# Awaiting the last five stores behind the end of the context, on semaphores of their own

## The chip, the cores and the metric

One core of a Trainium2 chip. The metric is the device time of one execution in microseconds, as a median of several executions. "Span" is the time from the first to the last instruction of the kernel in a trace; the device time is 1.3 to 1.8 us longer.

## The reference, cut to what matters

```python
W_adapted    = W + scale * (lora_A @ lora_B)              # 256 x 256
W_final      = W_adapted / sqrt(sum(W_adapted**2, 0) + 1e-8) * m
y            = x.reshape(-1, 256) @ W_final               # 32768 x 256, fp32 in and out
```

x and y have 33.55 MB each, so 67.1 MB must move between HBM and the core.

## The kernel before

The work is cut into 8 blocks of 4 MB. SyncE issues the loads and the stores; five buffers are shared by loads and stores (the result of a block overwrites its x). GpSimd rounds x to bf16, TensorE transposes it and multiplies, VectorE and ScalarE copy results. Everything stands in one critical section of the tile framework, and the engines keep in step by semaphores, counters that one engine or a transfer raises and another waits for. A transfer of x or y raises its semaphore 16 times; it has "landed" when the sixteenth increment is there. A barrier is a meeting point: no engine passes it before all have come. SyncE's stream, cut to the loads and stores of x:

```python
    ctx.enter_context(tc.tile_critical())          # line 54; closed when the function returns
    ...
    for b in range(XBUFS):                         # XBUFS = 5
        load_x(b)

    for b in range(NBLK):                          # NBLK = 8
        nc.sync.wait_ge(sem("done"), b + 1)        # ScalarE has written block b
        nc.sync.dma_start(out=rows(out_flat, b), in_=x_bufs[b % XBUFS][:]).then_inc(
            sem(f"store{b}"), 16)
        if b >= 1 and b - 1 + XBUFS < NBLK:
            nc.sync.wait_ge(sem(f"store{b - 1}"), 16)
            load_x(b - 1 + XBUFS)
    for b in range(NBLK - XBUFS, NBLK):            # the last five stores
        nc.sync.wait_ge(sem(f"store{b}"), 16)      # line 130
    ...
    with _tile.TileContext(nc) as tc:              # line 303; its exit adds the closing barriers
        tile_dora_forward_kernel(tc, *args)
```

So all stores have landed before the section is closed; then its barrier runs, then the context's: two barriers over all engines with a clear of the used semaphores between them.

Of the kernel before, what the change touches and what calls it, by code (L numbers as in the profile page):

```python
# [11 lines left out]
def kernel(  # L12
# [10 lines left out]
    nc = tc.nc  # L23
# [15 lines left out]
    NBLK = N // BLK  # L39
# [3 lines left out]
    XBUFS = 5  # L43
# [7 lines left out]



    ctx.enter_context(tc.tile_critical())

    def sb(name, shape, dtype):
        return ctx.enter_context(nc.sbuf_tensor(name, shape, dtype))
# [31 lines left out]
    n2_ps = y_ps[1][:, 0, :]  # L89
    mb_ps = y_ps[1][:, 2, :]  # L90

    sems = {}

    def sem(name):
        if name not in sems:
            sems[name] = tc.alloc_semaphore(name)
        return sems[name]
# [5 lines left out]
    def load_x(b):  # L103
        nc.sync.dma_start(out=x_bufs[b % XBUFS][:], in_=rows(x_flat, b)).then_inc(
            sem(f"load{b}"), 16
        )
# [14 lines left out]
    for b in range(NBLK):  # L121
# [4 lines left out]
        if b >= 1 and b - 1 + XBUFS < NBLK:  # L126
            nc.sync.wait_ge(sem(f"store{b - 1}"), 16)
            load_x(b - 1 + XBUFS)
    for b in range(NBLK - XBUFS, NBLK):
        nc.sync.wait_ge(sem(f"store{b}"), 16)  # L130


    nc.gpsimd.memset(zeros[:], 0.0).then_inc(sem("pool"), 1)
# [10 lines left out]
    for g in range(NCH):  # L144
        b, c = divmod(g, CH)
# [51 lines left out]
    for g in range(NCH):  # L197
        b, c = divmod(g, CH)
# [73 lines left out]
            product(c)  # L272


# [1 line left out]
_INS = ['x', 'W', 'lora_A', 'lora_B', 'm', 'scale']  # L276
_OUTS = [((16, 2048, 256), 'float32')]
# [30 lines left out]
```

## Time and profile before

| | before |
|---|---|
| device time, median | 166.26 us (166.16 to 166.46) |
| span of the profiled run | 164.3 us |
| traffic | 33.85 MB read, 33.55 MB written, 410 GB/s |
| last work of a compute engine | 139.6 us |
| last landing of a store | 162.80 us |

The page of the kernel before: the span, busy tenths of ScalarE and of the DMA engines in 40 slices, and the chain of work that ended last.

```profile
span 164.3 us, 2075 instructions
...
ACT  3010077577578577576000675027800377000000
...
DMA  5998999989999999999999999999999999999960
...
## 4 chain that ended last, share of the span: by engine, by line
PE 1%; ACT 1%; issue 0%
```

The DMA engines are busy from the second slice on, to the last but one; the compute engines have nothing left in the last six slices. The chain of this page stops at ScalarE's last copy, because it follows work of engines and not stores. The same in three stretches of the tail (the columns are named in the second line):

```profile
core 0 of [0], span 164.3 us
core 0: us, PE busy (x) PEld busy (x) DVE busy (x) ACT busy (x) POOL busy (x), PEclk, DMA share, GB/s
139.00:150.00 11.00, 0.00 (x0) 0.00 (x0) 0.00 (x0) 0.60 (x1) 0.00 (x0) 0.69 1.01 438
150.00:160.00 10.00, 0.00 (x0) 0.00 (x0) 0.00 (x0) 0.00 (x0) 0.00 (x0) 0.50 0.90 387
160.00:164.30 4.30, 0.00 (x0) 0.00 (x0) 0.00 (x0) 0.00 (x0) 0.00 (x0) 0.50 0.05 23
```

Up to 160 us the store stream is the whole matter, and after it come 4.3 us in which almost nothing moves. The waits of SyncE's queue in two windows (who waited for whom; us in total, how often, the longest; SPq and PEq are the instruction queues of SyncE and TensorE). From 139 to 150 us:

```profile
SPq L123 <- ACTq L205: 19.8, 1, 19.8
```

And from 150 us on:

```profile
SPq L130 <- DMA out_dram<-x_sb: 22.8, 2, 13.1
SPq L303 <- PEq L303: 0.8, 2, 0.6
```

Line 130 is the wait for the stores; line 303, the closing barriers, comes after it. What lies behind the last landing is too short for the page, so here is an extract of the trace's own records (start and end in us, engine, instruction, line; many left out):

```
162.799           last of the 16 increments of the last store
162.816 162.844   SyncE   semaphore wait (two of the stores)             130
162.889 162.921   SyncE   branch, with the wait for another store        109
163.044 163.061   SyncE   semaphore: the section's barrier begins         54
163.335 163.348   SyncE   the section's barrier ends                      54
163.610 163.661   TensorE semaphore: first barrier of the context ends   303
163.771 164.014   GpSimd  range clear of the semaphores                  303
164.258 164.309   TensorE semaphore: second barrier of the context ends  303
164.544 .. 165.069  nine updates of semaphore 2 (the runtime)
164.968 .. 165.633  resets of all semaphores (the runtime)
165.857 .. 166.215  nine updates of semaphore 2 (the runtime)
```

That the updates of semaphore 2 are the runtime's is from the Trainium skill, "Runtime: NRT & Kernel Launch", section "Semaphores 0–2 are reserved", which calls number 2 the sync barrier. The trace agrees so far as it goes: the kernel uses no such semaphore, and the updates come before its first instruction (the last of them within 0.001 us of it) and after its last.

Two of the 16 increments of the last store come late: fourteen are there by 160.31, the last two at 162.55 and 162.80.

### The profile page before, as it was taken

Reading aid. Unit: us, or ns where it says so; the run is one execution under the profiler, and the core shown is the slowest. Engines: PE = TensorE matmul, PEld = TensorE weight load, DVE = VectorE, ACT = ScalarE, POOL = GpSimd, SP = SyncE. Lnnn points to the kernel's source line nnn. Section 1 sums busy time; section 2 is a strip of 40 time slices with the busy share of each in tenths; the row PEclk is TensorE's granted clock in tenths of the full one; section 3 lists DMA queues with packets and bytes.
Section 4 is the critical chain, followed back from the end, with each engine's and each line's share of the span. In section 5 each row is a group of like instructions: output and inputs, shape, how many; then the busy total and the mean of one; then the engine's idle time right before and its main releaser. Section 6 shows DMA issues by size and latency. Waiting matters only on the chain. (4 is left out here: it accounts for less than half of the span.)

```text
span 164.3 us, 2075 instructions
## 1 busy us (share of the span) xinstructions
PE 99.7 (61%) x778; PEld 83.9 (51%) x778; DVE 51.2 (31%) x76; ACT 66.8 (41%) x67; POOL 66.2 (40%) x70
## 2 busy tenths in 40 slices
PE   1260899899899898994009993399704996000000
PEld 0120698798798796992007891279603895000000
DVE  0439355354453554451003450045301352000000
ACT  3010077577578577576000675027800377000000
POOL 1006859587785885800039600693007920000000
PEclk9999999999999999999555799579995799955555
DMA  5998999989999999999999999999999999999960
GB/s 199 415 479 383 499 391 415 479 383 495 399 399 359 399 479 401 439 439 399 479 407 439 447 399 457 433 423 455 407 431 439 423 463 399 439 447 407 471 295 16
DMA packets 2630, 67.45 MB, mean 410 GB/s; under 512 B 433, under 2 KB 450, under 8 KB 578
## 3 DMA queue, kind: packets, MB, share of 16 engines
q1 hardware_dynamic: 2448, 67.37, 95.9%
q10 hardware_dynamic: 178, 0.03, 0.1%
q8 instruction: 1, 0.02, 0.0%
q14 instruction: 3, 0.02, 0.0%
HBM read 33.85 MB, written 33.55 MB: 410 GB/s over the span
## 5 line engine op out<-in xcount | busy, mean ns | idle before, releaser
L150 POOL CAST xb<-x_sb 128x1024 bf16<-128x1024 f32 x64 | 65.5, 1049 | 65.2 <-DMA x_sb<-in_x_dram 50.6
L201 ACT COPY x_sb<-y_ps 128x1024 f32<-128x1024 f32 x64 | 64.8, 1013 | 64.5 <-PE y_ps L258 64.5
L258 PE MATMUL y_ps<-w_final,xt 128*128 128x256 bf16 x512 | 69.9, 282 | 3.9 <-PEq L235 3.6
L184 DVE COPY xt<-xt_ps 128x512 f32<-128x512 f32 x64 | 43.9, 691 | 77.1 <-PE xt_ps L246 77.1
L246 PE MATMUL xt_ps<-identity,xb 128*128 128x128 f32 x256 | 41.8, 295 | 28.4 <-PEq L235 28.4
L258 PEld LDWEIGHTS y_ps<-w_final,xt 128*128 128x128 bf16 x512 | 50.7, 101 | 14.7 <-issue 8.3
L246 PEld LDWEIGHTS xt_ps<-identity,xb 128*128 128x128 f32 x256 | 32.7, 153 | 31.4 <-issue 30.7
L223 PE MATMUL y_ps<-sq,ones 128*128 128x256 f32 x4 | 2.1, 674 | 1.6 <-DVE sq L169 1.6
L194 ACT ACTIVATE norm<-y_ps,eps_col 128x256 f32<-128x256 f32 x1 | 0.5, 474 | 5.9 <-PE y_ps L223 5.9
L212 PE MATMUL y_ps<-identity,a_nat 128*16 128x128 f32 x2 | 0.6, 396 | 3.6 <-DMA a_nat<-in_lora_A_dram 3.6
L180 DVE TENSOR_TENSOR w_final<-wam,rnorm 128x256 bf16<-128x256 f32 x2 | 2.3, 1200 | 0.0
L223 PEld LDWEIGHTS y_ps<-sq,ones 128*128 128x128 f32 x4 | 1.2, 323 | 2.3 <-DVE sq L169 2.1
L192 ACT ACT_TABLE_LOAD x1 | 1.3, 1283 | 2.4 <-issue 2.4
L212 PEld LDWEIGHTS y_ps<-identity,a_nat 128*16 128x16 f32 x2 | 0.1, 88 | 3.6 <-issue 3.6
L177 DVE RECIPROCAL rnorm<-norm 128x256 f32<-128x256 f32 x1 | 1.7, 1745 | 0.0
L171 DVE COPY m_all<-y_ps 128x256 f32<-128x256 f32 x1 | 0.4, 425 | 3.3 <-PE y_ps L228 3.3
L160 DVE CAST b_bf<-b_nat 16x256 bf16<-16x256 f32 x1 | 0.3, 281 | 3.6 <-DMA b_nat<-in_lora_B_dram 3.6
L216 PE MATMUL y_ps<-b_bf,aT 16*128 16x256 bf16 x2 | 0.6, 402 | 1.3 <-DVE aT L162 1.3
L228 PE MATMUL y_ps<-m_row,ones 1*128 1x256 f32 x2 | 1.2, 710 | 0.0
L216 PEld LDWEIGHTS y_ps<-b_bf,aT 16*128 16x128 bf16 x2 | 0.1, 104 | 1.8 <-DVE aT L162 1.8
L165 DVE SCALAR_TENSOR_TENSOR wa<-y_ps,w_nat 128x512 f32<-128x512 f32 x1 | 0.7, 692 | 0.8 <-PE y_ps L216 0.8
L228 PEld LDWEIGHTS y_ps<-m_row,ones 1*128 1x128 f32 x2 | 0.5, 308 | 0.7 <-issue 0.7
(12 smaller groups left out, 3.2 us busy)
## 6 DMA issues: line engine op xcount, KB each, us to landing
x_sb<-in_x_dram SPq DMA_DIRECT2D x8, 4096.0 KB, 29.3
out_dram<-x_sb SPq DMA_DIRECT2D x8, 4096.0 KB, 34.1
w_nat<-in_W_dram SPq DMA_DIRECT2D x1, 256.0 KB, 2.9
a_nat<-in_lora_A_dram ACTq DMA_DIRECT2D x1, 16.0 KB, 2.6
b_nat<-in_lora_B_dram ACTq DMA_DIRECT2D x1, 16.0 KB, 3.5
m_row<-in_m_dram ACTq DMA_DIRECT2D x1, 1.0 KB
```

The costliest lines, as they stand in the source:

```text
L150: nc.gpsimd.tensor_copy(out=xb_bufs[g % NXB][:], in_=x_bufs[b % XBUFS][:, c * J : (c + 1) * J, :],).then_inc(sem("rounded"), 1)
L165: nc.vector.scalar_tensor_tensor(out=wa[:], in0=ab_ps, scalar=float(scale), in1=w_nat[:], op0=ALU.mult, op1=ALU.add).then_inc(dv, 1)
L177: nc.vector.reciprocal(out=rnorm[:], in_=norm[:]).then_inc(dv, 1)
L180: i = nc.vector.tensor_mul(out=w_final[:, t], in0=wam[:, t], in1=rnorm[:])
L184: nc.vector.tensor_copy(out=xt_bufs[g % NXT][:].rearrange("p r t -> p (r t)").bitcast(FP32), in_=xt_ps[g % 4][:],).then_inc(sem("copied"), 1)
L192: nc.scalar.activation(out=warm[:], in_=eps_col[:], func=AF.Sqrt)
L201: nc.scalar.copy(out=x_bufs[b % XBUFS][:, c * J : (c + 1) * J, :], in_=y_ps[g % 2][:]).then_inc(sem("room"), 1)
L212: i = nc.tensor.transpose(aT_ps[:, t * P : (t + 1) * P], a_nat[:, t, :], identity[:])
L223: i = nc.tensor.matmul(n2_ps, ones[:], sq[:, t, :], start=(t == 0), stop=(t == KC - 1))
L228: nc.tensor.matmul(mb_ps, ones[0:1, :], m_row[:], start=True, stop=True).then_inc(pe, 1)
L246: i = nc.tensor.transpose(xt_ps[c % 4][:, j * P : (j + 1) * P], xb_bufs[c % NXB][:, j, :].bitcast(FP32), identity[:],)
L258: i = nc.tensor.matmul(y_ps[c % 2][:, j, :], xt_bufs[c % NXT][:, j * P : (j + 1) * P, t], w_final[:, t, :], start=(t == 0 and (j % (J // 2 ...
```

## The change

The intent: let the closing barriers run while the last stores travel, and have SyncE alone wait for the stores, behind all barriers. The context would clear and free semaphores of its own when it closes, so these five come from outside it and SyncE clears them.

```diff
-    ctx.enter_context(tc.tile_critical())
+    critical = ExitStack()
+    critical.enter_context(tc.tile_critical())
 ...
-    sems = {}
+    late = [nc.alloc_semaphore(f"store{b}") for b in range(NBLK - XBUFS, NBLK)]
+    sems = {f"store{b}": late[b - NBLK + XBUFS] for b in range(NBLK - XBUFS, NBLK)}
 ...
-    for b in range(NBLK - XBUFS, NBLK):
-        nc.sync.wait_ge(sem(f"store{b}"), 16)
 ...
+    critical.close()
+    tc.close()
+    tc.compile()
+    for s in late:
+        nc.sync.wait_ge(s, 16)
+        nc.sync.sem_clear(s)
```

## The prediction

> **What bounds the kernel now.** The DMA engines. The slices of the page show a DMA share of 0.9 to 1.0 from 5 us to 160 us; the stages view gives 1.01 and 438 GB/s in 139 to 150 us, with nothing left to compute. The traffic is 33.85 MB in and 33.55 MB out. The chain of waits on the page ends at 139.6 us, at the last ScalarE copy, because it does not follow stores; what really ends last is the store stream behind it. The DMA landings in the trace: the last store is issued at 139.66 and its sixteen increments arrive at 159.39 to 162.80 us (fourteen by 160.31, two stragglers 2.2 us later).
>
> **The tail, from the raw instruction and semaphore records.** Landing 162.80; SyncE's wait ends 162.84, its branch 162.92; the critical section's barrier (line 54) 163.04 to 163.35; first all-engine barrier (line 303) to 163.66; GpSimd clears the semaphore range 163.77 to 164.01; second barrier to 164.309, the end of the span. So 1.51 us lie between the last landing and the last instruction, all serial, all on the critical path. The Trainium skill, "Runtime: NRT & Kernel Launch", section "Semaphores 0-2 are reserved", says that semaphore 2 is the runtime's sync barrier; the trace has its updates at 164.54 to 165.07, then resets of all semaphores from 164.97 to 165.63, then again at 165.86 to 166.22. That part is behind the kernel and stays.
>
> **What the change removes, adds, moves.** No byte, no compute. SyncE leaves its stream right after issuing the last store (139.99), so the 1.4 us of closing barriers run at about 140.1 to 141.6 us, under the stores. What is left behind the last landing is one wait and one clear on SyncE. The wait took 0.044 us from landing to end of instruction; single semaphore instructions of SyncE take 17 to 32 ns and follow at about 60 ns. Estimate from these: last instruction at 162.80 + 0.04 + 0.08 = 162.92 us. The first four waits and clears are over long before (store 14 lands at 153.14). Saving in the span: 1.39 us.
>
> There should be a little more outside the span. In the old tail semaphore 2 waits about 0.17 us on its third hop (0.205 us against 0.034 to 0.044 elsewhere): a late engine. From the order of the resets (the group 207 to 255 first, at 164.97) I infer that SyncE is the turning point of this barrier. With the four others already there, only SyncE's own arrival counts. Estimate: SyncE's update about 0.25 us after its last instruction (Tensor's first took 0.235), where it was 0.59 us before: another 0.2 to 0.35 us. Total about 1.65 us.
>
> **Predicted:** 166.26 - 1.65 = 164.6 us, range 164.2 to 165.2; within 2% almost certainly (0.98), faster by over 2% 0.01, slower by over 2% 0.01. In the ratio: about 1% faster.
>
> **What would show each step right.** Span 162.8 to 163.1. The DMA queue's own waits: no wait for PEq late in the trace, the wait for the last store still at 162.8 and now the end. The records: line 54's and the closing line's barriers at 140 to 142 us. Landings of the last five stores unchanged within 0.3 us; DMA slices unchanged. Semaphore 2: hops without the 0.2 us gap.
>
> **What would make it wrong.** If SyncE's drain in the barriers waits for its outstanding DMAs, the barriers stay behind the landing and nothing is gained (166.2). No record here shows a drain with DMAs of its own queue in flight. If the clear on SyncE is as long as GpSimd's range clear (0.24 us), each costs and I lose 0.2 us. If SyncE's exit after its last instruction is slow, the extra outside the span is absent: 164.9.

## The result, and the profile after

The changed kernel takes 164.46 us (median, 164.38 to 164.72), the kernel before in the same rounds 166.35 us. The ratio is 0.989, interval 0.9873 to 0.9907. That is 1.9 us, or 1.1%: within 2%, as predicted, but clear of noise.

The page after, same lines:

```profile
span 163.1 us, 2077 instructions
...
ACT  3010278577576775773000774006740257300000
...
DMA  5999998998999999999999999999999999999990
```

The waits of SyncE's queue, again from 139 to 150 us. Line 281 holds the late waits and clears, line 278 is `tc.compile()`, where the barriers now are:

```profile
SPq L126 <- ACTq L206: 19.7, 1, 19.7
SPq L281 <- DMA out_dram<-x_sb: 1.5, 1, 1.5
SPq L278 <- PEq L278: 0.7, 2, 0.5
```

And from 150 us on:

```profile
SPq L281 <- DMA out_dram<-x_sb: 19.3, 2, 9.7
```

The barriers (0.7 us of waiting, 2 times) have changed windows: they stand ahead of the long wait for the stores, where before they stood behind it. The records of the tail:

```
140.785 140.802   SyncE   semaphore: the section's barrier begins         55
140.863 140.919   SyncE   drain in that barrier                           55
142.006 142.057   TensorE semaphore: second barrier of the context ends  278
142.292 .. 142.575  four of the nine updates of semaphore 2
163.039           last of the 16 increments of the last store
163.056 163.081   SyncE   clear, with the wait in the same instruction   281
163.198 .. 163.362  the other five updates of semaphore 2
164.148 .. 164.504  nine updates of semaphore 2
```

Two things have left the path behind the landing: the kernel's own barriers, as intended, and four of the nine updates of the runtime's next barrier, which now stand 20 us earlier. SyncE's first drain behind the issue of the last store took 56 ns, with three stores in flight for up to 22 us more: it does not wait for them. (Before, with none in flight, it took 7 ns; but the three drains that follow it here, with the same stores in flight, take 7 ns too, and so does the first one of e7_last_only below, with one store in flight. So the 49 ns are not shown to come from the stores.)

### The profile page after: what moved, and what is told of

Same layout as the page of the kernel before. It is cut to its first block, busy times and chain, and to the rows that moved or that the text cites. A ratio compares the mean times of both kernels' runs of the same rounds, so it can differ in the third digit from the quotient of the medians.

```text
span 163.1 us, 2077 instructions
## 1 busy us (share of the span) xinstructions
PE 100.2 (61%) x778; PEld 83.9 (51%) x778; DVE 49.7 (30%) x76; ACT 66.8 (41%) x67; POOL 65.4 (40%) x70
## 5 line engine op out<-in xcount | busy, mean ns | idle before, releaser
L151 POOL CAST xb<-x_sb 128x1024 bf16<-128x1024 f32 x64 | 64.7, 1041 | 66.7 <-DMA x_sb<-in_x_dram 56.1
L247 PE MATMUL xt_ps<-identity,xb 128*128 128x128 f32 x256 | 42.3, 297 | 29.3 <-PEq L236 29.3
L175 DVE TENSOR_TENSOR wam<-wa,m_all 128x256 f32<-128x256 f32 x2 | 0.8, 422 | 0.0
L181 DVE TENSOR_TENSOR w_final<-wam,rnorm 128x256 bf16<-128x256 f32 x2 | 0.8, 422 | 0.0
```

The lines of the kernel that those rows point to most:

```text
L151: nc.gpsimd.tensor_copy(out=xb_bufs[g % NXB][:], in_=x_bufs[b % XBUFS][:, c * J : (c + 1) * J, :],).then_inc(sem("rounded"), 1)
L175: i = nc.vector.tensor_mul(out=wam[:, t], in0=wa[:, t], in1=m_all[:])
L181: i = nc.vector.tensor_mul(out=w_final[:, t], in0=wam[:, t], in1=rnorm[:])
L247: i = nc.tensor.transpose(xt_ps[c % 4][:, j * P : (j + 1) * P], xb_bufs[c % NXB][:, j, :].bitcast(FP32), identity[:],)
```

## The experiments

Each kernel ran beside the kernel before on the same chip, in five rounds. The last landing scatters from run to run by some tenths of a us, and with it the time. The figures to compare finely are therefore the distances from the last landing, read from each run's profile: to the kernel's last instruction, and to the runtime's last update of semaphore 2. Each row has one profile.

| kernel | last landing | landing to last instruction | landing to last update | median | before, same rounds | ratio (interval) |
|---|---|---|---|---|---|---|
| before | 162.80 | 1.510 | 3.416 | 166.35 | | |
| changed | 163.04 | 0.042 | 1.465 | 164.46 | 166.35 | 0.989 (0.9873 to 0.9907) |
| e0_after (changed, again) | 162.80 | 0.041 | 1.465 | 164.12 | 166.12 | 0.9879 (0.986 to 0.9897) |
| e13_after_again (changed, again) | 162.86 | 0.042 | 1.469 | 164.17 | 166.17 | 0.988 (0.9865 to 0.9895) |
| e1_inside | 162.89 | 1.293 | 3.200 | 165.97 | 166.12 | 0.9977 (0.9956 to 0.9997) |
| e3_barrier_back | 162.63 | 0.297 | 2.202 | 164.71 | 166.12 | 0.9915 (0.9896 to 0.9933) |
| e4_tensor_waits | 162.99 | 0.085 | 1.830 | 164.63 | 166.12 | 0.9904 (0.9887 to 0.9921) |
| e5_no_clear | 162.89 | 0.045 | 1.471 | 164.20 | 166.12 | 0.9875 (0.986 to 0.989) |
| e6_clears20 | 162.84 | 1.183 | 2.609 | 165.40 | 166.12 | 0.9957 (0.9943 to 0.9971) |
| e7_last_only | 162.73 | 0.041 | 1.473 | 164.16 | 166.12 | 0.988 (0.9865 to 0.9896) |
| e12_inc_behind_waits | 162.83 | 1.434 | 3.339 | 166.20 | 166.17 | 1.0008 (0.9993 to 1.0023) |
| e11_early_w_x0 | 162.63 | 0.042 | 1.468 | 163.83 | 166.17 | 0.9857 (0.984 to 0.9873) |
| e10_early_loads | 190.93 | 0.042 | 1.468 | 191.90 | 166.12 | 1.1535 (1.1516 to 1.1555) |

My theory before these runs: the gain is nothing but order. What SyncE and the barriers do behind the last landing counts in full; what is moved ahead of it is free; the stream itself does not change. Rivals are named with each run.

**The changed kernel again.** No edit, run in two groups as a yardstick.

> The changed kernel again, as the yardstick of this group. Both theories: 164.3 to 164.8 us, span about 163.1. Also read here: is the last landing again 0.2 us later than in the kernel before (163.04 against 162.80), or was that chance? My theory: chance, within 0.3 us either way, because the barriers move no bytes.

> The changed kernel once more, as the yardstick for this group: 164.0 to 164.5 us, with 1.46 us from the last landing to the runtime's last barrier update, as in both profiles of it so far (1.465, 1.465).

The distances from the landing repeat to 0.004 us. The last landing was 162.80 and 162.86 us, so the 0.24 us by which the first profile of the changed kernel landed later was chance: over all profiles of this stream (without the two with early loads) it lies between 162.63 and 163.04 us.

**The waits at the old place, all else as changed (e1_inside).**

```diff
             load_x(b - 1 + XBUFS)
+    for s in late:
+        nc.sync.wait_ge(s, 16)
+        nc.sync.sem_clear(s)
 ...
     tc.compile()
-    for s in late:
-        nc.sync.wait_ge(s, 16)
-        nc.sync.sem_clear(s)
```

> The private semaphores and the clears stay, but SyncE waits at the old place, inside the critical section; the close of the context is unchanged. My theory (the gain is only the order of the barriers and the landing): back to the kernel before or 0.1 us over it for the clears, 166.2 to 166.6 us. Rival (the gain comes from the semaphores being others, or from closing the section and the context by hand): near 164.5 us.

The waits of SyncE's queue in this kernel from 150 us on; line 134 holds the waits and clears, line 281 the barriers:

```profile
SPq L134 <- DMA out_dram<-x_sb: 19.3, 2, 9.7
SPq L281 <- PEq L281: 0.7, 2, 0.5
```

The barriers are behind the landing again, and nearly all of the gain is gone: 165.97 us. The rival (other semaphores, closing by hand) falls as the main cause. But the run is not 0.1 us slower than the kernel before, as I had expected, but 0.15 us faster by the medians and 0.216 us by the distance to the last update. So a small part of the gain is not the order of barriers and landing. The records show where: in this kernel the barrier of the section begins 0.074 us after the landing (the clear that carries the wait ends 0.047 us after it), in the kernel before 0.245 us after it, because a branch with another wait and a pause of 0.12 us stand between. From there to the last instruction it is 1.219 against 1.265 us; GpSimd's range clear takes 0.207 instead of 0.243 us, with five semaphores fewer to clear, which is most of that. (With one fewer, in e7_last_only, it takes 0.226 us, with ten fewer, in e11_early_w_x0, 0.182.)

**Is it the branch? (e12_inc_behind_waits.)** The kernel before, with one instruction more:

```diff
     for b in range(NBLK - XBUFS, NBLK):
         nc.sync.wait_ge(sem(f"store{b}"), 16)
+    nc.sync.sem_inc(sem("spare"), 1)
```

> The kernel before, with one more instruction: SyncE increments a spare semaphore behind its last waits, inside the section. In the kernel before the last of the five waits rode on a branch (162.889 to 162.921) and the section's barrier began 0.12 us after it; with the waits on their own instructions at the same place the way from the last landing to the end was 0.217 us shorter (1.293 against 1.510). My theory: that is the branch, which is only there to carry a wait; with an instruction to carry it, the way is 0.15 to 0.2 us shorter in spite of the added instruction, about 166.0 us. Rival (private semaphores or clears did it): unchanged or 0.05 us longer.

The branch went from the records, and the section's barrier began 0.166 us after the landing instead of 0.245: 0.08 us shorter, half of what I expected, and too little to show in the time (166.20 against 166.17 us). From there to the last instruction it is 1.268 us here and 1.265 in the kernel before, so a second profile agrees with its only one. The other half was not the branch. In both kernels the compiler joined the five waits in pairs and put semaphores that had been reached for long on an instruction behind the one that waits for the last store (S119 is the semaphore of the last store; S114, S116 and S117 are those of the first three of the five):

```
before:               162.816 162.844 SyncE wait (S119, S116); 162.889 162.921 SyncE branch, wait (S114)
e12_inc_behind_waits: 162.847 162.875 SyncE wait (S119, S117); 162.914 162.942 SyncE increment, wait (S114, S116)
```

In the changed kernel each wait rides on its own clear, in order, and none follows the last. That accounts for the remaining 0.09 us; this sum is read from three profiles, and not tried by itself.

**A barrier back (e3_barrier_back).**

```diff
         nc.sync.sem_clear(s)
+    nc.all_engine_barrier()
```

> One all-engine barrier is put behind the late waits. My theory: the barrier itself costs about 0.34 us in the span (first barrier of the closing line before: 163.38 to 163.66, and a drain), and since all engines are now late again for the runtime's barrier, its earlier hops come back: SyncE's hop came 0.54 us after the last instruction before, 0.12 us now, so 0.43 us more. Together +0.75 us: about 165.2 us. Rival (only the kernel's span counts, the runtime's barrier costs the same however the engines arrive): +0.34 us, 164.8 us.

The distance to the last update grew from 1.465 to 2.202 us, by 0.737 us: 0.255 in the span, and 0.482 between the kernel's last instruction and the runtime's last update. The medians differ by 0.59 us; the landing of this profile was 0.17 us earlier than that of e0_after. The rival, that only the span counts, falls: the part behind the kernel is the larger one.

**TensorE waits instead of SyncE (e4_tensor_waits).**

```diff
-        nc.sync.wait_ge(s, 16)
-        nc.sync.sem_clear(s)
+        nc.tensor.wait_ge(s, 16)
+        nc.tensor.sem_clear(s)
```

> The late waits and clears run on TensorE instead of SyncE, nothing else. My theory (in the runtime's barrier the engines arrive one after another and SyncE is the turning point, TensorE the first): the span grows by at most 0.1 us, but four more hops lie behind the landing: about 0.33 us more than the changed kernel, 164.8 us. Rival (which engine waits does not matter): the changed kernel's time, within 0.1 us.

The kernel's last instruction came 0.043 us later after the landing, the runtime's last update 0.365 us later; the medians differ by 0.51 us, some of it a later landing. The nine updates of semaphore 2, counted from the last landing:

```
changed:         -20.75 -20.71 -20.51 -20.46 | 0.159 0.204 0.242 0.276 0.323
e4_tensor_waits:   0.280 0.314 0.353 0.396 0.419 0.520 0.560 0.594 0.641
```

With SyncE as the late engine, four updates are done long before; with TensorE none is. So in the runtime's barrier TensorE comes first and SyncE fifth, at the turning point, and it matters which engine is late. SyncE is the cheaper of the two that were tried. The Trainium skill, "Runtime: NRT & Kernel Launch", section "The ~15µs preamble/postamble breakdown", gives about 355 ns for this way over the five engines (44 ns a hop, eight hops, a hop being the step from one update to the next), for the barrier ahead of a kernel. Here the nine updates ahead of the kernel before take 0.372 us, and the nine of e4_tensor_waits 0.361 us, with single hops of 0.023 to 0.101 us. The sum agrees; the hops are uneven.

**Without the clears, and with twenty more (e5_no_clear, e6_clears20).**

```diff
e5_no_clear:
         nc.sync.wait_ge(s, 16)
-        nc.sync.sem_clear(s)
e6_clears20:
         nc.sync.sem_clear(s)
+    for _ in range(20):
+        nc.sync.sem_clear(late[-1])
```

> The five late waits without the five clears. My theory: only the last clear lies behind the last landing, and it carries its wait in the same instruction, so a wait alone takes the same 0.03 us: the changed kernel's time within 0.1 us. Rival (the clears cost something each, as GpSimd's range clear of 0.2 us): 0.2 us or more faster than the changed kernel.

> Twenty more clears on SyncE behind the last landing. In the changed kernel two clears that waited for nothing began 0.069 us apart. My theory: everything that SyncE does behind the last landing counts in full: 20 x 0.069 = +1.4 us, about 165.8 us. Rival (the clears run ahead, or the runtime's own work covers them): about 164.5 us.

Without the clears the distance to the last update is 1.471 against 1.465 us: the one clear that lies behind the landing costs nothing, since it carries the wait. Twenty more cost 1.144 us to the last update, and 1.2 us of time (165.40 us against 164.17 of e13_after_again on the same chip): they count in full, at 0.057 us each. The expected 0.069 was too much; it was read from the distance of two clears that each also had a wait to check, where these had none; that this makes the difference was not tried. (The kernel without clears is correct; the runtime's resets follow, as in every run.)

**How many stores must be late? (e7_last_only.)**

```diff
-    late = [nc.alloc_semaphore(f"store{b}") for b in range(NBLK - XBUFS, NBLK)]
+    late = [nc.alloc_semaphore(f"store{b}") for b in range(NBLK - 1, NBLK)]
 ...
             load_x(b - 1 + XBUFS)
+    for b in range(NBLK - XBUFS, NBLK - 1):
+        nc.sync.wait_ge(sem(f"store{b}"), 16)
```

> Only the last store is awaited behind the context; the four before it are awaited at the old place, so the barriers begin when store 14 has landed, at about 153 us instead of 140.8. My theory: they need 1.3 us and still have almost 10 us of cover, so the time is that of the changed kernel within 0.1 us. Rival (all five stores have to be late, or barriers and stores disturb one another while they overlap): a difference of 0.2 us or more, with the last landing moved.

(The "store 14" of the recorded texts is the last store but one, store6.) Same time (164.16 us against 164.17 in e13_after_again on the same chip), same distances. The second barrier of the context ended at 154.5 us here instead of 141.7 (e0_after). One late store is enough, since 8.3 us of waiting are left behind the barriers:

```profile
SPq L133 <- DMA out_dram<-x_sb: 9.7, 1, 9.7
SPq L283 <- DMA out_dram<-x_sb: 8.3, 1, 8.3
SPq L280 <- PEq L280: 0.7, 2, 0.6
```

Since the last landing did not move with the barriers' place (162.73 us), neither do barriers and stores disturb one another by an amount that can be seen here.

**The same thought at the front (e10_early_loads, then e11_early_w_x0).** If work of the DMA engines can overlap the closing barriers, the first loads may overlap the opening ones. In e10 all five loads of x are issued ahead of the context, on semaphores of their own:

```diff
+        for k in range(5):
+            nc.sync.dma_start(out=nc.early_x[k][:], in_=<block k of x>).then_inc(
+                nc.early_sems[f"load{k}"], 16)
         with _tile.TileContext(nc) as tc:
 ... (inside the context; the making of buffers and semaphores is left out)
-    for b in range(XBUFS):
-        load_x(b)
```

> The mirror image at the front, to try for a faster kernel: the first five loads of x are issued ahead of the context, on semaphores of their own, so SyncE issues its first transfer at about 0.70 us instead of 0.94, and x goes ahead of W. Where the DMA engines bound everything, the whole stream should move up by 0.2 to 0.4 us: 164.1 to 164.3 us. If the stream is not what counts, or W coming later delays the first store: no gain, or a loss.

It took 191.9 us. W is issued inside the context and so came to stand behind 20 MB of x. From its page: the slices of the DMA engines, what VectorE waited for (a group of instructions: busy us, mean ns, then the idle time before it and what ended that), and the issue of W (KB, us to landing):

```profile
DMA  6999999999800000795998989999999999999993
...
L165 DVE SCALAR_TENSOR_TENSOR wa<-y_ps,w_nat 128x512 f32<-128x512 f32 x1 | 0.7, 691 | 31.6 <-DMA w_nat<-in_W_dram 31.6
...
w_nat<-in_W_dram SPq DMA_DIRECT2D x1, 256.0 KB, 49.4
```

W landed 49.4 us after its issue (2.9 us in the kernel before), at 52.88 us, just after the fifth block of x (52.26). Until then there was no weight, no product and no store. Then the loads were done and no buffer was free, and the DMA engines stood idle for five slices, until the weights and the first block's result were made and the first store was issued at 77.3 us (30.9 in the kernel before). The Trainium skill, "DMA: Bandwidth & Descriptors", section "Queues, rings and completion order", says that on each DMA engine descriptors (the single pieces of a transfer) are consumed in the order of the ring; this run agrees: W's first increment came at 52.41 us, behind the last of the fifth block. I had put "W coming later" among the possible losses and had not counted how much later.

In e11 the order of the queue is kept. W and the first block of x on SyncE and the three small loads on ScalarE go ahead of the context; the other four blocks stay inside.

```diff
+        load(nc.sync, w_nat[:], ..., "load_w")
+        load(nc.sync, x_bufs[0][:], ..., "load0")
+        load(nc.scalar, a_nat[:], ..., "load_a")      # and b_nat, m_row
         with _tile.TileContext(nc) as tc:
 ...
-    for b in range(XBUFS):
+    for b in range(1, XBUFS):
         load_x(b)
```

> The mirror image at the front once more, with the order of the queue kept: W and the first block of x on SyncE, the three small loads on ScalarE, ahead of the context; the other four blocks inside it, as before. (With all five blocks ahead, W landed at 52.9 us behind them and the kernel took 191.9 us.) SyncE's first transfer should be issued at about 0.73 us instead of 0.94. If the DMA stream bounds everything from its first packet on, all landings move up by 0.2 us: 163.8 to 164.1 us. If the first microseconds of the stream have slack, no gain.

SyncE's first transfer was issued at 0.738 us instead of 0.944, the first packet of the queue moved at 1.746 instead of 1.98, and the last landing was at 162.63. That alone lies within the scatter (e3_barrier_back had 162.63 too), but all 16 landings of x and y came earlier, by 0.08 to 0.23 us than in the profile before and by 0.12 to 0.36 us than in those of e0_after and e13_after_again, from the first load on. The time was 163.83 us (163.64 to 163.98), beside 164.17 us (164.03 to 164.36) of the changed kernel in the same rounds. The two ranges do not meet, though the intervals of the two ratios do: it is the fastest kernel of this study, in its group by about 0.3 us, and faster than both kernels compared here.

A version with the waits between the end of the section and the end of the context was built too. The check found a deadlock in it, and the shares of the section's barrier and of the context's two are not measured apart.

## Why the prediction was right

- *The DMA stream bounds the kernel, and the change leaves it as it is.* Right. The busy slices are the same within a tenth, and the last landing, 162.63 to 163.04 us over all profiles of this stream, has no order by kernel.
- *1.51 us lie between the last landing and the last instruction, all of it on the path.* Right; 0.04 us are left (predicted 0.12). The prediction put a clear behind the wait; it is one instruction. Saved: 1.468 us in place of 1.39.
- *A little more is saved outside the span, 0.2 to 0.35 us.* Right in its mechanism, too small in size. From the last instruction to the runtime's last update it was 1.906 us before and 1.423 after: 0.483 us. The mis-sized term was SyncE's own arrival: I took TensorE's 0.235 us for it, and it took 0.117 us (163.081 to 163.198). Before it had been 0.542 us (164.309 to 164.851), where the prediction says 0.59. So 0.425 of the 0.483 us are SyncE's update, and 0.054 the four hops behind it, which took 0.218 us before and 0.164 after. That SyncE is the turning point was inferred from the order of the resets; e4_tensor_waits shows it for the two engines tried.
- *Total about 1.65 us, 164.6 us.* The sum in the records is 1.951 us, the medians say 1.89 in the first comparison and 2.00 and 2.00 in the two repeats. The first result, 164.46 us, lies in the range by luck: it was helped by a landing 0.24 us late in its profile. The repeats, at 164.12 and 164.17, are just under the range, beside a kernel before of 166.12 and 166.17.
- *SyncE's drain might wait for its transfers.* It does not: 56 ns with stores in flight.
- *Semaphore 2: hops without the 0.2 us gap.* This sign did not come. The step to the third update of the barrier still takes 0.205 us (142.326 to 142.531). It costs nothing only because it now lies 20 us ahead of the landing; it is gone (0.039 us) only in e4_tensor_waits, where the first engine comes last. (The other steps in the old tail are 0.024 to 0.099 us, not "0.034 to 0.044".)
- What the prediction did not see: of the 1.951 us, 0.216 are not barriers moved (e1_inside has them without the move). By the records they are a branch with a wait, a second instruction for waits already met, and a shorter range clear; of these only the branch was tried by itself. The rest divides into 1.251 us of barriers and 0.484 us behind the kernel (1.293 - 0.042 and 3.200 - 1.293 - 1.423).

## What to carry to other kernels

When a kernel ends on a store, look at what lies between that store's last landing and the last instruction: barriers there can run while the store travels. Of the two engines tried as the late one, SyncE, at the turning point of the runtime's barrier, cost less than TensorE, and one wait that carries its own clear was enough. The gain here was 2 us of 166, and one late store is enough if it travels longer than the barriers take. Moving transfers ahead at the front works by the same reasoning, but the order in the queue decides: a small load that everything waits for must not fall behind large ones.

## What the Trainium skill lacked or had wrong

- "Runtime: NRT & Kernel Launch", section "The ~15µs preamble/postamble breakdown", does not say in which order the engines arrive, nor that it matters which one is late: with SyncE late 0.117 us passed to its update and five updates were left, with TensorE late all nine, 0.365 us more to the last update.
- The same table gives about 1.5 us each for the barrier and the resets behind the kernel; here the resets took 0.67 us (164.968 to 165.633). The barrier was over 0.760 us after the kernel's last instruction (its updates took 0.525 us, 164.544 to 165.069) with all engines arriving together, and 0.281 us after it with four engines early.
- No page says what a drain on an engine that issues transfers waits for: not for its stores in flight. With three of SyncE's own outstanding, the drain next behind the issue took 56 ns and the three after it 7 ns each; with none outstanding, all took 7 ns.
- No page has the cost of semaphore instructions on SyncE in a row (0.057 us per clear), nor that a clear which carries a wait costs no more than the wait (0.042 us from the landing to the last instruction with the clear, 0.045 without).
- "DMA: Bandwidth & Descriptors", section "Latency and other measured facts", says that two DMA engines, 7 and 15, are usually slower, and as a best guess, not certain, ties this to transfers issued from GpSimd. Here all transfers came from SyncE and ScalarE, and yet one or two of the sixteen increments come late, in the kernel before in the last store (fourteen by 160.31 us, two at 162.55 and 162.80) and in every transfer of x and y from the second load on (that one: fifteen by 23.38 us, the last at 24.79). Which DMA engines they are the kept traces do not say, and the cause stays open; it is now a longer stretch than anything behind the landing.
